# 128 unused bytes ahead of the tiles of h: where the normalised activations begin in SBUF, in a two-layer trunk on one core

## The chip, the cores and the metric

The kernel runs on one core of a Trainium2 chip. The metric is the device time of one execution in microseconds (us), the median over runs.

## What is computed

Two decoder layers over 256 positions of 1024 channels, in float32. Each layer is a half-step SwiGLU FFN, a mixer, and a second half-step FFN; each sublayer has an RMS norm whose output is scaled and shifted by vectors that come from a conditioning row. Layer 0 mixes by causal pooling, layer 1 by attention to K and V that are computed once from the output of layer 0. Since SEQ is 256 and a block has 256 positions, the attention is plain causal attention over one block.

```python
def swiglu(h, w_in, w_out):
    g, u = jnp.split(h @ w_in, 2, axis=-1)          # w_in 1024 x 5632
    return (jax.nn.silu(g) * u) @ w_out             # w_out 2816 x 1024
...
x = x + 0.5 * (1.0 + g)[:, None, :] * swiglu(modulate(rms_norm(x, n), sh, sc), w_in, w_out)   # four times
...
k, v = jnp.split(hn @ w_kv, 2, axis=-1)             # once, after layer 0; hn is "h of shared K/V"
```

## The kernel before, in words

Everything is transposed: channels lie on the 128 partitions, the 256 positions on the free axis, so that h is a tile of 128 x 8 x 256 (`KT` = 8 blocks of channels).

**Three matmuls for one product.** Every operand of a large product is split into a rounded part `hi` and the rest `lo` (ACT casts, L167 and L128; DVE subtracts, L168 and L129), and `mm3` issues three matmuls for each product. The first operand after the output is the stationary one (128 columns, "the weights" of a matmul, loaded anew for every matmul), the second the moving one (256 columns):

```python
    def mm3(o, wh, wl, xh, xl, start, stop):
        i = nc.tensor.matmul(o, wh, xh, ...)             # L255
        nc.tensor.matmul(o[:, 0:T], wh, xl, ...)         # L258
        nc.tensor.matmul(o, wl, xh, ...)                 # L259
```

**The four FFNs.** The weights stream from HBM into raw tiles and are split into tiles of the pool `wp`: stream A (2048 wide: the first product) and stream B (1024 wide: the second). A *gu unit* (`gstep`, L461 ff.) is 48 matmuls: two halves of 8 blocks of channels, three matmuls each; all 24 of a half add into one half of a PSUM tile, and the moving tile (a slice of `hhi` or `hlo`) changes with each block. A *y unit* (`ystep`, L478 ff.) is 24 matmuls: 8 output blocks, three each, with one moving tile pair `acth`, `actl` throughout, and the output changes after every three. `ffn_rest` alternates them: in most of an FFN one gu unit, then one y unit. The first channels of FFNs 2 to 4 are computed ahead from x itself (`gu<-xah`, `gu<-xal`, 258 columns, tiles `kxhi`, `kxlo`), while the norm is being worked out. At the end of an FFN its last y products (96 matmuls) run without gu units between them.

In layer 1, `pj` are the K and Q products (moving tile `hkvh`, `hkvl` or `hhi`, `hlo`; stationary tiles of stream A), `v` the V products (here `hkvh`, `hkvl` are stationary and the tiles of stream A move), `s`, `att` the products of the attention itself, and `y<-hhi` in L1000 the output projection (stationary tiles of stream B, moving `hhi`, `hlo`, which hold the attention's output by head), in the same order of outputs as a y unit.

DVE and ACT do the splits, the norms, the activations and the modulation's dot products (`mod_dot`, L263, from tiles `rawX`, `rawA`, `kxhi`, `kxlo` that are loaded from `in_ada`). SP issues the loads. TensorE's and SP's order is the program's; some stretches of DVE and ACT are ordered by hand, the rest by a scheduler.

**Where tiles lie.** Pools are laid out one after the other in each partition of SBUF, in the order in which they are opened, and tiles in a pool in the order in which their tags are first asked for. Two small tiles that nothing reads stand for room alone:

```python
    ax = ctx.enter_context(tc.tile_pool(name="ax", bufs=8))     # acth, actl
    cp = ctx.enter_context(tc.tile_pool(name="cp", bufs=1))     # constants, x, kxhi, kxlo
    wp = ctx.enter_context(tc.tile_pool(name="wp", bufs=2))     # raw, hi, lo of the two streams
    tp = ctx.enter_context(tc.tile_pool(name="tp", bufs=2))
    hp = ctx.enter_context(tc.tile_pool(name="hp", bufs=1))     # hhi, hlo
    ...
    ax.tile([P, 16], F32, tag="room0", name="room0", bufs=1)
    ...
    cp.tile([P, 16], F32, tag="room1", name="room1")
```

After `hp` come `xp` (`rawX` and the pooling matrix `at`, in layer 0) and in its place later `ap` (`hkvh`, `hkvl`, and the attention's `qh`, `ql`, `ph`, `pl`). In the built program the first bytes of the tiles that TensorE reads are, modulo 256:

| tile | pool | first byte mod 256 | minus the stream's tiles |
|---|---|---|---|
| hi, lo of streams A and B | wp | 160 | 0 |
| acth, actl (all 16 buffers) | ax | 192 | +32 |
| kxhi (xah, kh) / kxlo (xal, kl) | cp | 32 / 96 | +128 / +192 |
| hhi, hlo | hp | 64 | +160 |
| hkvh, hkvl, qh, ql, ph, pl | ap | 64 | +160 |

Every slice that a matmul takes of a stream tile begins a multiple of 512 bytes into it, and every slice of `hhi`, `hlo`, `acth`, `actl`, `hkvh`, `hkvl` a multiple of 512 bytes into that. So the last column holds for each single matmul of its kind, at any block of channels. (Slices of `kxhi` and `kxlo` lie 1032 bytes apart, so theirs grows by 8 with each block.) In a `v` product the roles are changed: what moves lies at 160 and what is stationary at 64, +96.

Of the kernel before, what the change touches and what calls it, by code (L numbers as in the profile page):

```python
# [7 lines left out]
F32 = mybir.dt.float32  # L8
# [5 lines left out]
P = 128  # L14
# [72 lines left out]
def trunk(ctx: ExitStack, tc: tile.TileContext, xin, cin, small, ada, kvada, win0a, win1a, win0b,  # L87
# [7 lines left out]
    hp = ctx.enter_context(tc.tile_pool(name="hp", bufs=1))  # L95
# [2 lines left out]


    ax.tile([P, 16], F32, tag="room0", name="room0", bufs=1)  # L100

    uid = [0]

# [1047 lines left out]
```

## Time and profile before

| | |
|---|---|
| median of 3 runs | 906.83 us (906.48 to 907.52) |
| the profiled execution's own time | 906.3 us |
| its span, first to last instruction | 904.2 us |
| TensorE (PE) busy | 890.9 us, 99% |
| its weight loads (PEld) | 884.3 us, 98% |
| DVE / ACT / POOL busy | 717.4 / 452.5 / 49.2 us |
| HBM read | 238.11 MB, 265 GB/s over the span |

Matmuls are pipelined: a row gives one a duration of 0.28 us, while the next starts about 0.12 us after it. The time that a stretch of matmuls takes is therefore read from starts: the start of the first matmul after it minus the start of its first, divided by their number. This is called the *pitch* below. In the timeline, the columns are the start in us from the span's start, the duration in us, engine, line, operation, output<-inputs, shapes and count.

### The profile page before, as it was taken

The page shows a single profiled execution, that of the slowest core. Times are in us where ns is not written, and L with a number is a line of the kernel's source. Part 1 is how long each engine was busy: PE and PEld are TensorE (multiplying, and loading weights), DVE is VectorE, ACT ScalarE, POOL GpSimd, SP SyncE. Part 2 cuts the span into 40 slices and gives each one's busy share as a digit, 9 for nine tenths or more (in the row PEclk, how much of TensorE's full clock was granted, in tenths as well). Part 3 has the DMA queues.
Part 4 walks back from the last instruction along what each step waited for, and adds up shares of the span by engine and source line. Part 5 has one row for each costly group of instructions (what it writes and reads, how often), then busy time and mean ns, then how long its engine had stood idle before and what let it go on. Part 6 is the DMA issues. An engine that isn't in the chain of part 4 may idle for free.

```text
span 904.2 us, 17826 instructions
## 1 busy us (share of the span) xinstructions
PE 890.9 (99%) x7398; PEld 884.3 (98%) x7398; DVE 717.4 (79%) x1212; ACT 452.5 (50%) x721; POOL 49.2 (5%) x52
## 2 busy tenths in 40 slices
PE   6999999999999999999999999999999999999998
PEld 4999999999999999999999999999999999999998
DVE  5988988878998878869998888789887894665553
ACT  3455344328734444457554443456676674343431
POOL 0000000002000000000000000034431100000000
PEclk9999999999999999999999999999999999999999
DMA  9987998784799998454989899664534376645421
GB/s 354 420 328 288 418 370 345 275 327 147 279 421 400 365 328 323 167 199 165 366 313 391 323 370 358 233 234 184 175 106 132 112 274 253 236 165 205 165 71 47
DMA packets 41699, 240.32 MB, mean 266 GB/s; under 512 B 4625, under 2 KB 5009, under 8 KB 20370
## 3 DMA queue, kind: packets, MB, share of 16 engines
q1 hardware_dynamic: 41618, 239.18, 69.7%
q8 instruction: 58, 0.95, 0.4%
q14 instruction: 23, 0.19, 0.1%
HBM read 238.11 MB, written 1.05 MB: 265 GB/s over the span
## 4 chain that ended last, share of the span: by engine, by line
PE 93%; DVE 4%; DMA 1%; ACT 1%; POOL 1%; issue 0%; DVEq 0%; SPq 0%; POOLq 0%
PE gu L259 18%; PE gu L255 18%; PE gu L258 18%; PE y L258 10%; PE y L255 10%; PE y L259 10%; DVE lo L168 1%; PE gu L720 1%; PE pj L255 1%; PE pj L258 1%; PE pj L259 1%; DMA rawA<-in_ada_dram 1%; PE z L796 1%; DVE rawA L263 1%; POOL r L343 1%
## 5 line engine op out<-in xcount | busy, mean ns | idle before, releaser
L167 ACT CAST hi<-raw 128x1024 fp32r<-128x1024 f32 (+1 forms) x322 | 302.1, 973 | 338.1 <-PE gu L258 224.4
L168 DVE TENSOR_TENSOR lo<-raw,hi 128x1024 fp32r<-128x1024 f32 (+1 forms) x322 | 355.4, 1131 | 135.9 <-ACT hi L167 132.6
L259 PE MATMUL gu<-hhi,lo 128*128 128x256 f32 x1248 | 351.9, 282 | 0.0
L255 PE MATMUL gu<-hhi,hi 128*128 128x256 f32 x1248 | 351.9, 282 | 0.0
L258 PE MATMUL gu<-hlo,hi 128*128 128x256 f32 x1248 | 351.9, 282 | 0.0
L259 PEld LDWEIGHTS gu<-hhi,lo 128*128 128x128 f32 x1248 | 237.5, 190 | 0.2 <-DVE lo L168 0.2
L258 PEld LDWEIGHTS gu<-hlo,hi 128*128 128x128 f32 x1248 | 237.3, 190 | 0.0
L255 PEld LDWEIGHTS gu<-hhi,hi 128*128 128x128 f32 x1248 | 237.2, 190 | 0.0
L255 PE MATMUL y<-acth,hi 128*128 128x256 f32 x704 | 196.4, 279 | 0.0
L259 PE MATMUL y<-acth,lo 128*128 128x256 f32 x704 | 196.3, 279 | 0.0
L258 PE MATMUL y<-actl,hi 128*128 128x256 f32 x704 | 196.3, 279 | 0.0
L255 PEld LDWEIGHTS y<-acth,hi 128*128 128x128 f32 x704 | 132.6, 188 | 0.0
L258 PEld LDWEIGHTS y<-actl,hi 128*128 128x128 f32 x704 | 132.5, 188 | 0.0
L259 PEld LDWEIGHTS y<-acth,lo 128*128 128x128 f32 x704 | 132.3, 188 | 0.0
L263 DVE CUSTOM_DVE_ANT_0 rawX<-rawX,cb 128x1024 f32<-128x1024 f32 x80 | 94.6, 1219 | 0.1
L416 ACT ACTIVATE sl<-gu 128x256 f32<-128x256 f32 x79 | 29.4, 377 | 39.3 <-PE gu L259 37.3
L417 DVE TENSOR_TENSOR sl<-gu,sl 128x256 f32<-128x256 f32 x79 | 32.7, 417 | 14.0 <-ACT sl L416 14.0
L255 PE MATMUL gu<-xah,hi 128*128 128x258 f32 x144 | 41.3, 287 | 0.0
L259 PE MATMUL gu<-xah,lo 128*128 128x258 f32 x144 | 40.7, 282 | 0.0
L258 PE MATMUL gu<-xal,hi 128*128 128x256 f32 x144 | 40.7, 282 | 0.0
L128 ACT CAST acth<-sl 128x256 fp32r<-128x256 f32 x79 | 31.8, 405 | 11.4 <-DVE sl L417 9.9
L129 DVE TENSOR_TENSOR actl<-sl,acth 128x256 fp32r<-128x256 f32 x79 | 32.8, 418 | 1.6 <-ACT acth L128 1.6
(146 smaller groups left out, 1000.0 us busy)
## 6 DMA issues: line engine op xcount, KB each, us to landing
raw<-in_win1b_dram SPq DMA_DIRECT2D x57, 1024.0 KB, 5.3
raw<-in_wout_dram SPq DMA_DIRECT2D x88, 512.0 KB, 5.9
rawX<-in_ada_dram SPq DMA_DIRECT2D x34, 1024.0 KB, 8.6
raw<-in_win1a_dram SPq DMA_DIRECT2D x14, 1024.0 KB, 9.7
rawA<-in_ada_dram SPq DMA_DIRECT2D x12, 1024.0 KB, 6.9
kxhi<-in_ada_dram SPq DMA_DIRECT2D x11, 1024.0 KB, 7.5
kxlo<-in_ada_dram SPq DMA_DIRECT2D x10, 1024.0 KB, 8.7
raw<-in_win0b_dram SPq DMA_DIRECT2D x12, 768.0 KB, 4.2
```

What stands on the lines that cost most here:

```text
L128: i = nc.scalar.copy(hi, src)
L129: nc.vector.tensor_tensor(lo, src, hi.bitcast(F32), op=ALU.subtract)
L167: return [(lambda a=a, b=b: after_anchor(nc.scalar.copy(hi[:, a:b], raw[:, a:b])), lambda a=a, b=b: nc.vector.tensor_tensor(lo[:, a:b], ra ...
L168: lambda a=a, b=b: nc.vector.tensor_tensor(lo[:, a:b], raw[:, a:b], hi[:, a:b].bitcast(F32), op=ALU.subtract)) for a, b in cut]
L255: i = nc.tensor.matmul(o, wh, xh, start=start, stop=False, skip_group_check=True)
L258: nc.tensor.matmul(o[:, 0:T], wh, xl, start=False, stop=False, skip_group_check=True)
L259: nc.tensor.matmul(o, wl, xh, start=False, stop=stop, skip_group_check=True)
L263: i = nc.vector.tensor_tensor_reduce(out=v, in0=v, in1=cb, scale=1.0, scalar=0.0, op0=ALU.mult, op1=ALU.add, accum_out=mb[:, col:col + 1])
L343: nc.gpsimd.tensor_tensor(r, ms, nhalf[:, :n], op=ALU.pow)
L416: nc.scalar.activation(sl, ps[:, 0:T], AF.Silu)
L417: nc.vector.tensor_mul(sl, ps[:, T:2 * T], sl)
L720: nc.tensor.matmul(g0[j][:, half * T:(half + 1) * T], w0[:, (2 * j + half) * P:(2 * j + half + 1) * P], h0, start=(half == 0), stop=False, ...
```

## The change

One unused tile of 32 float32 in each partition (128 bytes) is asked for first in the pool `hp`:

```diff
     ax.tile([P, 16], F32, tag="room0", name="room0", bufs=1)
+    hp.tile([P, 32], F32, tag="room2", name="room2")
 
     uid = [0]
```

`hhi`, `hlo` and everything in `xp` and `ap` begin 128 bytes later: at 192 modulo 256, where they began at 64. Nothing else moves. On every engine the instructions, their order and what they wait for are the same as before; below L99 the line numbers are larger by one.

| tile | minus the stream's tiles, before | after |
|---|---|---|
| hhi, hlo, hkvh, hkvl | +160 | +32 |
| acth, actl | +32 | +32 |
| kxhi / kxlo | +128 / +192 | the same |
| a `v` product (moving minus stationary) | +96 | +224 |

In the attention, `s` (moving kh or kl, stationary qh or ql) and `att` (moving ph or pl, stationary acth or actl) change by 128 as well: 48 matmuls each.

## Rows read from the trace of the kernel before

**Rows 1.** The page: PE's line, and the chain that ended last by engine.
```profile
PE 890.9 (99%) x7398; PEld 884.3 (98%) x7398; DVE 717.4 (79%) x1212; ACT 452.5 (50%) x721; POOL 49.2 (5%) x52
...
PE 93%; DVE 4%; DMA 1%; ACT 1%; POOL 1%; issue 0%; DVEq 0%; SPq 0%; POOLq 0%
```
**Rows 2.** Waits of the weight loads for split weights: us in total, times, longest.
```profile
PEld gu L259 <- DVE lo L168: 0.2, 1, 0.2
```
**Rows 3.** Timeline of PE, FFN 2: a gu unit begins, a y unit, a gu unit.
```profile
299.60 0.28 PE L255 MATMUL gu<-hhi,hi 128*128 128x256 f32 x1
...
305.36 0.28 PE L255 MATMUL y<-acth,hi 128*128 128x256 f32 x1
...
308.16 0.28 PE L255 MATMUL gu<-hhi,hi 128*128 128x256 f32 x1
```
**Rows 4.** Timeline of PE, output projection: two blocks of 24 and what follows each.
```profile
684.48 0.28 PE L255 MATMUL y<-hhi,hi 128*128 128x256 f32 x1
...
687.34 0.27 PE L982 MATMUL pT<-ident,p 128*128 128x128 f32 x1
...
689.08 0.28 PE L255 MATMUL y<-hhi,hi 128*128 128x256 f32 x1
...
691.90 0.28 PE L255 MATMUL att<-ph,acth 128*128 128x256 f32 x1
```
**Rows 5.** Timeline of PE: first y unit and next gu unit, FFNs 2 and 3.
```profile
245.62 0.28 PE L255 MATMUL y<-acth,hi 128*128 128x256 f32 x1
...
248.42 0.28 PE L255 MATMUL gu<-hhi,hi 128*128 128x256 f32 x1
...
254.06 0.28 PE L255 MATMUL y<-acth,hi 128*128 128x256 f32 x1
...
434.34 0.28 PE L255 MATMUL y<-acth,hi 128*128 128x256 f32 x1
...
437.17 0.28 PE L255 MATMUL gu<-hhi,hi 128*128 128x256 f32 x1
...
442.87 0.28 PE L255 MATMUL y<-acth,hi 128*128 128x256 f32 x1
```
**Rows 6.** Timeline of PE: ends of FFN 1's first h block and of the steady stretches.
```profile
24.06 0.28 PE L255 MATMUL gu<-hhi,hi 128*128 128x256 f32 x1
...
74.40 0.28 PE L255 MATMUL y<-acth,hi 128*128 128x256 f32 x1
...
96.94 0.28 PE L255 MATMUL gu<-hhi,hi 128*128 128x256 f32 x1
...
193.74 0.28 PE L255 MATMUL y<-acth,hi 128*128 128x256 f32 x1
...
265.36 0.28 PE L255 MATMUL gu<-hhi,hi 128*128 128x256 f32 x1
...
393.76 0.28 PE L255 MATMUL y<-acth,hi 128*128 128x256 f32 x1
...
445.67 0.28 PE L255 MATMUL gu<-hhi,hi 128*128 128x256 f32 x1
...
582.63 0.28 PE L255 MATMUL y<-acth,hi 128*128 128x256 f32 x1
```
**Rows 7.** Timeline of PE: a block of 48 v products, and the first pj after it.
```profile
593.87 0.28 PE L255 MATMUL v<-hi,hkvh 128*128 128x256 f32 x1
...
599.61 0.28 PE L255 MATMUL pj<-hkvh,hi 128*128 128x256 f32 x1
```
**Rows 8.** Busy time by stretch, FFN 3: us, PE, PEld, DVE, ACT, POOL, PEclk, DMA share, GB/s.
```profile
446.00:582.00 136.00, 136.00 (x1146) 136.00 (x1145) 118.61 (x180) 60.61 (x86) 0.00 (x0) 1.00 0.87 332
```
**Rows 9.** DVE's dot products by tile (L263): duration ns min/median/max.
```profile
L263 DVE CUSTOM_DVE_ANT_0 rawX<-rawX,cb x80: 1207/1219/1226, 9.1 to 366.2; 128x1024 f32<-128x1024 f32 x80
L263 DVE CUSTOM_DVE_ANT_0 kxhi<-kxhi,cb x24: 1212/1218/1221, 268.1 to 807.0; 128x1024 f32<-128x1024 f32 x24
```

## The prediction, made before the run

> **What bounds the kernel.** I read the page first: PE is busy 99% of the span, and the chain that ended last is PE for 93% of it [rows 1]. Next the waits: over the whole run the weight loads wait 0.2 us for split weights [rows 2]. So the time is the number of matmuls times their pitch, and almost nothing else. The windows come third: in the FFN that loads the other engines most, PE is busy 136 of 136 us at the full granted clock (1.00, the 2.4 GHz level), DVE 118.61 of 136 (87%), DMA 0.87 [rows 8]. The change neither adds nor removes an instruction; it can only act through the pitch, so the timeline of PE is what the prediction rests on.
>
> There the reader sees two pitches. The gu unit from 299.60 to 305.36 has 48 matmuls: 5.76 us / 48 = 120.0 ns. The y unit behind it, to 308.16, has 24: 2.80 / 24 = 116.7 ns [rows 3]. Both have 256 moving columns, 128 stationary ones, and no wait. They differ in two ways: gu adds 24 times into one output with a new moving tile for each three, and its moving tile lies 160 bytes beyond the stationary one modulo 256, that of y 32.
>
> **Which of the two it is.** The attention's output projection separates them: it runs in the order of a y unit, but its moving tile is `hhi`, at +160. Its blocks of 24 take 687.34 − 684.48 = 2.86 us (119.2 ns) and 691.90 − 689.08 = 2.82 us (117.5 ns) [rows 4]. The gu units show the same two values where they are not at 120: 254.06 − 248.42 = 5.64 us / 48 = 117.5 ns in FFN 2, and 442.87 − 437.17 = 5.70 / 48 = 118.75 ns in FFN 3 [rows 5]. At +160, then, I see three levels, 117.5, about 119 and 120, for either order of work. At +32 I see two: 116.7 (245.62 to 248.42, 2.80 us / 24) and, in FFN 3's first y unit, 117.9 (434.34 to 437.17, 2.83 / 24) [rows 5]. So the pitch goes with the offset, not with the order of work, and with something that the stretch carries along, a phase between the two reads. FFN 1 and 2 enter in the low level of their offset, FFN 3 in the higher one (and FFN 4 likewise). From the third gu unit of each FFN on, after two changes between +160 and +32, every gu unit stands at 120.0 and every y unit at 116.7.
>
> A rule of the skill speaks against this reading. The Trainium skill, "SBUF — State Buffer", section "Who interferes with whom", says that PE has two independent SBUF read ports, one for the moving operand and one for the weight loads, and that PE never waits on anyone. By it an address could not matter and the time would stay. [Rows 4] disagree in so far as the same order of work runs slower at +160; what it would give here stands among the rivals.
>
> **The change part by part.** The new tile is never written, and costs no instruction. What it does is to put `hhi`, `hlo`, `hkvh`, `hkvl` at +32, where `acth` lies.
>
> (1) *Steady gu units.* The stretches run from 96.94 to 193.74 (10 gu units and 336 y matmuls: 480 × 120.0 + 336 × 116.7 ns = 96.8 us, as measured), 265.36 to 393.76 (15 units, 360 y: 128.4 us), and 445.67 to 582.63 (16 units, 384 y: 137.0 us) [rows 6]; FFN 4 is built as FFN 3. That is 480 + 720 + 768 + 768 = 2736 matmuls at 120.0. At 116.7 each saves 3.3 ns: −9.0 us.
>
> (2) *h blocks near an entry.* FFN 1's first block takes 74.40 − 24.06 = 50.34 us for 429 matmuls, 117.3 ns [rows 6]; at 116.7, −0.28. FFN 1 has 48 more at 117.5 and 48 at about 119 (−0.13), FFN 2 144 at 117.5 and 48 at about 119 (−0.21). FFNs 3 and 4 have 144 each at 118.75, and in the higher level of +32 (117.9) they save 0.12 each. Together −0.86.
>
> (3) *Layer 1's projections.* 384 `pj` and 192 `y<-hhi` matmuls, between 117.5 and 119.2 now [rows 4]: about 1 ns each, −0.6. The start of this stage hangs on DVE, not on PE, so I take half: −0.3.
>
> (4) *FFNs 3 and 4 stay in the level in which they enter.* Before, the shift between +160 and +32 moved them out of it after two units. After the change h and act lie at one offset, and nothing shifts. So I let FFN 3 and 4 run at 117.9 throughout: the 1536 steady gu matmuls save 2.1 ns and not 3.3 (+1.84), and their 960 later y matmuls rise from 116.7 to 117.9 (+1.15). This is my choice; the bounds follow from it.
>
> (5) *Products with an offset that no row shows*: 192 `v` (+96 to +224), 48 `s` and 48 `att`. The nearest row is `v` itself, 599.61 − 593.87 = 5.74 us / 48 = 119.6 ns [rows 7]. All rows of unpaused blocks lie between 116.7 and 120.0, so 288 matmuls may gain 2.9 ns or lose 0.4: −0.8 to +0.1. I take 0, since the nearest row lies at the upper end, and allow ±0.8.
>
> (6) *What else moves.* `rawX` begins 128 bytes later for its loads and for DVE's dot products. These take 1219 ns from `rawX` and 1218 from `kxhi`, which lies elsewhere modulo 256 [rows 9]: nothing. `xah` and `xal` stay.
>
> *Cover.* A steady gu and y pair shrinks from 8.56 to about 8.40 us. DVE's share in FFN 3 rises from 87 to 89%, that of DMA from 0.87 to 0.89 [rows 8], so I let neither take any of it back. Late next would be DVE's split of the weights, whose 0.2 us [rows 2] falls at a transition between stages.
>
> The sum: −9.03 − 0.86 − 0.3 + 1.84 + 1.15 = −7.2 us against the profiled execution's own 906.3 (span 904.2): 899.1. The median of the runs is 0.5 above that execution, so I give **899.6**.
>
> **The rivals.**
> - *All four FFNs in the low level.* Then (4) falls away and the entries of 3 and 4 save 0.35 more: −10.5, 896.3. For it: from the third unit on all y units stand at 116.7. Against: two of four enter at the higher level.
> - *All four in the higher level.* FFN 1 and 2 lose 1.2 ns on 1200 gu matmuls (1.4), on 2 × 528 y matmuls (1.3) and on their entries (0.9): −3.6, 903.2.
> - *No effect of the address.* If the 120 belongs to the work of a gu unit (24 adds into one output) and not to the offset, nothing moves: 906.8. [Rows 4] speak against it. It is also the result of the skill's rule on the two ports.
> - *Slower: y loses its level and gu gains nothing.* The place is the steady alternation. If y reaches 116.7 only because a gu unit at another offset hands over its phase, and h locks at 120 whatever its offset, then with one offset for both all 2112 y matmuls run at 117.9, 2.5 us more: 909.3. It decides if the steady gu pitch stays above 119.1 ns (2.5 us over 2736 matmuls is 0.9 ns). For it: FFN 3's first y unit at 117.9 [rows 5] before any such exchange. Against: FFN 2's first at 116.7.
> - *The feeds take it back.* If FFN 3, with DVE at 87%, kept its 137 us, its part of the sum (768 × 2.1 − 480 × 1.2 ns = 1.0 us) would be lost: 900.6, in the range.
> - *The tile doesn't move h.* The built program has h 128 bytes later, so I give this nothing.
>
> **How the numbers follow.** Forecast (some FFNs low, some high) 0.46; all low 0.25; all high 0.08; fed too slowly 0.04; no effect 0.10; slower 0.07. The range reaches from all low with the gain of (5), 896.3 − 0.8 = 895.5, to all high with its loss, 903.2 + 0.8 = 904.0; what is left out is no effect, slower, and a little beside them. A measurement of this kernel tells 0.2% (1.8 us) from no change. Faster by more: 0.46 + 0.25 + 0.08 + 0.04 = 0.83; same 0.10; slower 0.07.
>
> **What would show it.** In the timeline, a gu unit of FFN 2 should take 5.60 us (116.7 ns) or 5.66 (117.9) in place of 5.76, and the y unit beside it should be at the same pitch. FFN 3's steady 137.0 us should be about 135.8 if it is in the higher level, 134.4 if low; FFN 1's 96.8 should be 95.2. The count of matmuls, DVE's 1219 ns and the granted clock should not change. It is wrong if gu units stay at 120.0, if they take another pitch than 116.7 or 117.9, or if they reach it and PE then waits for DVE or DMA in steady stretches.

## The result, and the profile after

The changed kernel takes 896.96 us (median of 4 runs, 894.96 to 899.96) against 906.79 before (906.48 to 907.52): a ratio of 0.9893, 95% interval 0.9864 to 0.9922. Timed once more (v_after, below) it took 895.98 us (894.64 to 897.02), ratio 0.9883 (0.9866 to 0.9900). The forecast was 899.6 us in a range of 895.5 to 904.0, and faster with 0.83.

The profiled execution of the changed kernel took 894.96 us, the quickest of the first four; its span is 892.8 us where that of before was 904.2. First the page after: PE's line, and the chain by engine. They answer to [rows 1].

```profile
PE 879.4 (99%) x7398; PEld 873.0 (98%) x7398; DVE 717.1 (80%) x1212; ACT 453.0 (51%) x721; POOL 49.4 (6%) x52
...
PE 93%; DVE 4%; DMA 1%; ACT 1%; POOL 1%; issue 0%; DVEq 0%; SPq 0%; POOLq 0%
```

The same 7398 matmuls and 1212 DVE instructions, the same shares of the chain, 11.5 us less of PE. DVE's and ACT's busy time is unchanged within 0.5 us: nothing but the matmuls became cheaper.

The timeline of PE after, FFNs 1 to 4. The rows answer to [rows 3, 6]: FFN 1's first h block (first two rows), ends of the steady stretches, and in FFN 2 a gu unit, a y unit, a gu unit.

```profile
23.64 0.28 PE L256 MATMUL gu<-hhi,hi 128*128 128x256 f32 x1
...
73.69 0.28 PE L256 MATMUL y<-acth,hi 128*128 128x256 f32 x1
...
96.09 0.28 PE L256 MATMUL gu<-hhi,hi 128*128 128x256 f32 x1
...
191.29 0.28 PE L256 MATMUL y<-acth,hi 128*128 128x256 f32 x1
...
262.72 0.28 PE L256 MATMUL gu<-hhi,hi 128*128 128x256 f32 x1
...
287.92 0.28 PE L256 MATMUL gu<-hhi,hi 128*128 128x256 f32 x1
...
293.52 0.28 PE L256 MATMUL y<-acth,hi 128*128 128x256 f32 x1
...
296.32 0.28 PE L256 MATMUL gu<-hhi,hi 128*128 128x256 f32 x1
...
388.72 0.28 PE L256 MATMUL y<-acth,hi 128*128 128x256 f32 x1
...
440.30 0.28 PE L256 MATMUL gu<-hhi,hi 128*128 128x256 f32 x1
...
574.70 0.28 PE L256 MATMUL y<-acth,hi 128*128 128x256 f32 x1
...
743.00 0.28 PE L256 MATMUL gu<-hhi,hi 128*128 128x256 f32 x1
...
877.40 0.28 PE L256 MATMUL y<-acth,hi 128*128 128x256 f32 x1
```

FFN 4's steady stretch before, for which [rows 6] have no row:

```profile
751.86 0.28 PE L255 MATMUL gu<-hhi,hi 128*128 128x256 f32 x1
...
888.81 0.28 PE L255 MATMUL y<-acth,hi 128*128 128x256 f32 x1
```

The gu unit takes 293.52 − 287.92 = 5.60 us for 48 matmuls, 116.7 ns where it was 120.0; the y unit 2.80 us for 24, 116.7 ns as before. The steady stretches take 95.20, 126.00, 134.40 and 134.40 us. Against 96.80, 128.40 and 136.96 of before [rows 6], with FFN 4 before at 136.95, that is 9.1 us less. The span fell by 11.4. Of the other 2.3 us, 0.42 lie ahead of FFN 1's first h block (it begins at 23.64 and began at 24.06), where the moved tiles play no part; in v_after, the same kernel once more, the block began at 24.09, so these 0.42 us are no gain of the change. 0.43 lie between that and FFN 1's steady stretch, and 0.2, 0.3 and 0.9 in the three stretches between the steady ones.

Busy time in FFN 3's stretch after (us, PE, PEld, DVE, ACT, POOL, granted clock, DMA share, GB/s); it answers to [rows 8].

```profile
441.00:574.00 133.00, 133.00 (x1142) 133.00 (x1141) 118.08 (x179) 60.50 (x86) 0.00 (x0) 1.00 0.89 339
```

PE is still busy all of it, at the same granted clock (1.00), with DVE now at 118.08 of 133 (89%) and DMA at 0.89. The feeds took nothing back.

### The profile page after: what moved, and what is told of

Read it like the earlier page. It is cut to its first block, busy times and chain, and to the rows that moved or that the text cites. A ratio compares the mean times of both kernels' runs of the same rounds, so it can differ in the third digit from the quotient of the medians.

```text
span 892.8 us, 17826 instructions
## 1 busy us (share of the span) xinstructions
PE 879.4 (99%) x7398; PEld 873.0 (98%) x7398; DVE 717.1 (80%) x1212; ACT 453.0 (51%) x721; POOL 49.4 (6%) x52
## 4 chain that ended last, share of the span: by engine, by line
PE 93%; DVE 4%; DMA 1%; ACT 1%; POOL 1%; issue 0%; DVEq 0%; SPq 0%; POOLq 0%
PE gu L256 18%; PE gu L260 18%; PE gu L259 18%; PE y L259 10%; PE y L256 10%; PE y L260 10%; DVE lo L169 1%; PE gu L721 1%; PE pj L256 1%; PE pj L259 1%; PE pj L260 1%; DMA rawA<-in_ada_dram 1%; PE z L797 1%; DVE rawA L264 1%; POOL r L344 1%
## 5 line engine op out<-in xcount | busy, mean ns | idle before, releaser
L256 PE MATMUL gu<-hhi,hi 128*128 128x256 f32 x1248 | 348.4, 279 | 0.0
L260 PE MATMUL gu<-hhi,lo 128*128 128x256 f32 x1248 | 348.3, 279 | 0.0
L259 PE MATMUL gu<-hlo,hi 128*128 128x256 f32 x1248 | 348.2, 279 | 0.0
L260 PEld LDWEIGHTS gu<-hhi,lo 128*128 128x128 f32 x1248 | 234.6, 188 | 0.1
L256 PEld LDWEIGHTS gu<-hhi,hi 128*128 128x128 f32 x1248 | 234.6, 188 | 0.0
L259 PEld LDWEIGHTS gu<-hlo,hi 128*128 128x128 f32 x1248 | 234.6, 188 | 0.0
L264 DVE CUSTOM_DVE_ANT_0 rawX<-rawX,cb 128x1024 f32<-128x1024 f32 x80 | 94.6, 1219 | 0.4 <-DMA rawX<-in_ada_dram 0.4
L129 ACT CAST acth<-sl 128x256 fp32r<-128x256 f32 x79 | 31.9, 406 | 13.1 <-DVE sl L418 11.4
```

What stands on the lines that cost most here:

```text
L129: i = nc.scalar.copy(hi, src)
L256: i = nc.tensor.matmul(o, wh, xh, start=start, stop=False, skip_group_check=True)
L259: nc.tensor.matmul(o[:, 0:T], wh, xl, start=False, stop=False, skip_group_check=True)
L260: nc.tensor.matmul(o, wl, xh, start=False, stop=stop, skip_group_check=True)
L264: i = nc.vector.tensor_tensor_reduce(out=v, in0=v, in1=cb, scale=1.0, scalar=0.0, op0=ALU.mult, op1=ALU.add, accum_out=mb[:, col:col + 1])
```

## The experiments

Theory A: a matmul's pitch goes with the distance modulo 256 between the first bytes of its moving and its stationary tile, and at each distance has a few levels. Theory B: the gain comes from what lies behind h. Theory C: it comes from the address of h itself. The kernel before ran again beside each group of runs; a ratio compares the runs with those beside them, and is not the quotient of two medians of the table. Times from one run carry no interval. The offsets in the table are those from the tiles of the two weight streams, modulo 256; gu and y are the pitches in steady units of the four FFNs in the profiled execution.

| run | h | act | us (runs) | ratio to before | gu, ns | y, ns |
|---|---|---|---|---|---|---|
| before | 160 | 32 | 906.79 (4) | | 120.0 | 116.7 |
| the change | 32 | 32 | 896.96 (4) | 0.9893 (0.9864 to 0.9922) | 116.7 | 116.7 |
| v_after, the change again | 32 | 32 | 895.98 (4) | 0.9883 (0.9866 to 0.9900) | 116.7; FFN 2 117.8 | 116.7; FFN 2 117.8 |
| e1_h_only | 32 | 32 | 895.30 (4) | 0.9877 (0.9861 to 0.9894) | 116.7 | 116.7 |
| e2_kv_only | 160 | 32 | 906.88 (10) | 1.0003 (0.9993 to 1.0012) | 120.0; FFN 2 118.7 | 116.7 |
| e3_plus384 | 32 | 32 | 897.10 (1) | | 116.7 | 116.7 |
| e4_both160 | 160 | 160 | 905.69 (10) | 1.0004 (0.9987 to 1.0021) | FFN 1 120.0, others 118.7 | the same as gu |
| s_h0 | 0 | 32 | 911.94 (1) | | 119.9 | 118.0 |
| s_h64 | 64 | 32 | 893.80 (1) | | FFNs 1, 2 113.4; 3, 4 117.8 | 116.9, 117.1; 116.6 |
| s_h96 | 96 | 32 | 908.85 (1) | | 119.8 to 119.9 | 118.1 in FFN 1, 116.6 |
| s_h224 | 224 | 32 | 903.35 (1) | | 118.3 | 116.9 |
| b_64_64 | 64 | 64 | 896.68 (5) | 0.9914 (0.9879 to 0.9948) | 117.8 | 117.8 |
| b_64_192 | 64 | 192 | 897.57 (5) | 0.9912 (0.9884 to 0.9939) | 117.8 | FFN 1 113.5, others 117.6 to 117.7 |
| v_h64, s_h64 again | 64 | 32 | 894.63 (4) | 0.9864 (0.9847 to 0.9880) | FFNs 1, 2 113.4; 3, 4 117.8 | 116.9, 117.1; 116.6 |

**e1_h_only: h alone is moved.** From the changed kernel, a second unused tile behind h puts all that follows back to where it was modulo 256.

```diff
     hp.tile([P, 32], F32, tag="room2", name="room2")
...
             h = new_h("h")
+            hp.tile([P, 32], F32, tag="room3", name="room3")
```

> Only hhi and hlo lie at +32; a second unused tile behind them leaves hkvh, hkvl, rawX and the tiles of the attention where before had them modulo 256 (+160). Theory A (the offset between the moving and the stationary tile of a matmul sets its pitch): gu units of the four FFNs at 116.7 ns, or 117.9 in an FFN that falls into the higher level; the 192 pj matmuls on hkvh, hkvl stay at 117.4 to 118.8 and the v blocks near 119.8, as before; the time 0.5 to 1 us above the change, 896 to 900 us. Theory B (the gain comes from what lies behind h: the loads' tiles or the shared K/V): gu units stay at 120.0 and the time near 906.8.

895.30 us (894.49 to 895.79). The timeline of PE, FFN 2, and below it a block of 48 v products with the first pj behind it:

```profile
288.47 0.28 PE L256 MATMUL gu<-hhi,hi 128*128 128x256 f32 x1
...
294.07 0.28 PE L256 MATMUL y<-acth,hi 128*128 128x256 f32 x1
...
586.46 0.28 PE L256 MATMUL v<-hi,hkvh 128*128 128x256 f32 x1
...
592.21 0.28 PE L256 MATMUL pj<-hkvh,hi 128*128 128x256 f32 x1
```

gu units 5.60 us, 116.7 ns; v stays at 5.75 us / 48 = 119.8 ns, where the change has 118.3. The whole gain is there without shared K/V; the 0.5 to 1 us that I had put on shared K/V are not, and the time lies below the 896 to 900 that I expected. Theory B falls.

**e2_kv_only: the complement.** The unused tile behind h alone, from the kernel before.

```diff
             h = new_h("h")
+            hp.tile([P, 32], F32, tag="room3", name="room3")
```

> The complement: hhi and hlo stay at +160, everything behind them moves by 128 bytes as in the change. Theory A: gu units at 120.0 from the third of each FFN on, pj on hkvh, hkvl at 116.7 to 117.9 and v blocks near 118.3; the time 0 to 1 us under before, 905.8 to 906.8. Theory B: the time near 897.

906.88 us, ratio 1.0003 (0.9993 to 1.0012). The timeline of PE: a gu unit of FFN 2, one of FFN 3, and a block of v:

```profile
275.23 0.28 PE L255 MATMUL gu<-hhi,hi 128*128 128x256 f32 x1
...
280.93 0.28 PE L255 MATMUL y<-acth,hi 128*128 128x256 f32 x1
...
471.81 0.28 PE L255 MATMUL gu<-hhi,hi 128*128 128x256 f32 x1
...
477.57 0.28 PE L255 MATMUL y<-acth,hi 128*128 128x256 f32 x1
...
594.30 0.28 PE L255 MATMUL v<-hi,hkvh 128*128 128x256 f32 x1
...
599.98 0.28 PE L255 MATMUL pj<-hkvh,hi 128*128 128x256 f32 x1
```

In FFNs 1, 3 and 4 gu is at 5.76 us, 120.0 ns, as before. The v blocks did become shorter (5.68 us / 48 = 118.3 ns against 119.6 before [rows 7]), and three of the four pj blocks on hkvh fell to 116.6 to 116.8 (without the one gap of some 0.2 us that three of the blocks hold), yet the time did not move. The trace shows one reason: behind these products PE waits for POOL, before and after the change alike. The rows are those of the kernel before and of the change, with the wait in brackets:

```profile
634.25 0.65 PE L349 MATMUL rbk<-ident,r 128*128 128x128 f32 x4 [1.84 <-POOL r L343]
...
626.21 0.65 PE L350 MATMUL rbk<-ident,r 128*128 128x128 f32 x4 [2.09 <-POOL r L344]
```

From the start of FFN 3's last y products (582.63 and 574.70) to these rows it is 51.62 and 51.51 us: with the change the wait grew by 0.25 us and the stretch shrank by 0.11, so the wait takes most of what these products save.

One thing was not as expected: in FFN 2 gu stayed at 118.7 in every unit of this execution (5.70 us above), and never reached 120, although its units alternated between +160 and +32.

**e3_plus384: is the period 256?** 384 bytes in place of 128, so that h is 32 beyond the weights modulo 256 but 288 modulo 512.

```diff
-    hp.tile([P, 32], F32, tag="room2", name="room2")
+    hp.tile([P, 96], F32, tag="room2", name="room2")
```

> The unused tile has 384 bytes in place of 128: h is again 32 beyond the weights modulo 256, but 288 modulo 512 (the change has 32, the activations 288). Theory A with a period of 256 bytes: gu units at 116.7 (or 117.9 in an FFN), 895 to 900 us. Rival (period of 512 or more): gu units at another pitch than 116.7 or 117.9.

897.10 us in one run. The timeline of PE, a gu unit of FFN 2, and the window from 626 to 630 us (us, PE, PEld, DVE, ACT, POOL, granted clock, DMA share, GB/s):

```profile
288.48 0.28 PE L256 MATMUL gu<-hhi,hi 128*128 128x256 f32 x1
...
294.08 0.28 PE L256 MATMUL y<-acth,hi 128*128 128x256 f32 x1
...
626.00:630.00 4.00, 3.33 (x16) 3.33 (x17) 3.65 (x7) 3.11 (x5) 2.02 (x2) 0.58 0.74 262
```

5.60 us, 116.7 ns; gu and y are at 116.7 in all four FFNs. For this distance it makes no difference whether h lies 32 or 288 beyond. All FFNs are in the low level as in the first execution of the change, and yet the time is 2.1 us longer. 0.5 us lie ahead of FFN 1's first h block, and 1.6 in layer 1: there PE, after a wait of 2.0 us for POOL, runs at a mean granted clock of 0.58, for the most part at the lower of its two levels (1.2 GHz), and its matmuls start 0.21 us apart in place of 0.12. In the first execution of the change the same place, after a wait of 2.1 us, shows 1.00. So a time alone does not tell how many FFNs are in the high level.

**e4_both160: the distance or the address?** 128 more bytes behind the activations, from the kernel before. The weights and h move up by them: h comes to lie at 192 modulo 256, as in the change, but still 160 from the weights, and the activations now lie 160 from the weights too.

```diff
-    cp.tile([P, 16], F32, tag="room1", name="room1")
+    cp.tile([P, 48], F32, tag="room1", name="room1")
```

> From the kernel before, 128 more unused bytes behind the activations' tiles: acth, actl now lie at +160 from the weights, as h does; h itself, the weights and all else behind lie 128 bytes further up, with the same offsets among themselves. Theory A1 (the offset sets the levels, and only the alternation between two offsets drives the phase up to 120): gu and y units all stay at the level in which an FFN enters, 117.4 or 118.7; 901 to 907.5 us. Theory A2 (at +160 a stretch settles at 120 by itself): gu and y both at 120.0, 913 to 914 us. Theory C (it is the address of h itself, 192 modulo 256, not its distance from the weights): gu units at 116.7, 896 to 900 us.

905.69 us (903.83 to 910.42). The timeline of PE, FFN 1 (first two rows) and FFN 2:

```profile
119.21 0.28 PE L255 MATMUL gu<-hhi,hi 128*128 128x256 f32 x1
...
124.97 0.28 PE L255 MATMUL y<-acth,hi 128*128 128x256 f32 x1
...
294.86 0.28 PE L255 MATMUL gu<-hhi,hi 128*128 128x256 f32 x1
...
300.56 0.28 PE L255 MATMUL y<-acth,hi 128*128 128x256 f32 x1
...
303.40 0.28 PE L255 MATMUL gu<-hhi,hi 128*128 128x256 f32 x1
```

FFN 1: 5.76 us / 48 = 120.0 ns. FFN 2: gu 5.70 / 48 = 118.75, y 2.84 / 24 = 118.3 (118.7 over all its units). The address of h is the same as in the change and the pitch is not: theory C falls. The y units, at 116.7 for as long as their tile lay at +32, now run at the pitch of the gu units. That is the other half of the case for theory A: the order of work of a y unit does not make it quick. The median agrees with A1 (901 to 907.5) and not with A2 (913 to 914); three of the ten runs lie above A1's range, this execution (910.27) among them. In its detail A1 was wrong: FFN 1 sat at 120.0 without any alternation of offsets.

**s_h0, s_h64, s_h96, s_h224: other distances.** The unused tile has 96, 160, 192 and 64 bytes.

```diff
-    hp.tile([P, 32], F32, tag="room2", name="room2")
+    hp.tile([P, 24], F32, tag="room2", name="room2")
```

The others have 40, 48 and 16 in place of 24.

> The unused tile has 96 bytes: h and shared K/V begin exactly at the weights modulo 256 (offset 0), the activations stay at +32. What each offset gives was not known for this one. Theory A (each offset has its own few levels of pitch, +32 those at 116.7 and 117.9): gu units at some other level, between 116 and 126 ns, y units at 116.7 to 117.9; 895 to 925 us. Rival A' (only +160, half a period from +32, is slow): gu at 116.7, about 897 us.

> The unused tile has 160 bytes: h and shared K/V at +64, the activations at +32. Theory A: gu units at a level of their own between 116 and 122 ns; y units at 116.7 to 117.9; 895 to 912 us. Rival A': gu at 116.7, about 897 us.

> The unused tile has 192 bytes: h and shared K/V at +96. Before had the v products at this offset, in another role, at 119.8 ns. Theory A: gu units at 118 to 121 ns, 900 to 910 us. Rival A': gu at 116.7, about 897 us.

> The unused tile has 64 bytes: h and shared K/V at +224 (32 short of the weights). After the change the v products have this offset, in another role, at 118.3 ns. Theory A: gu units at 117 to 121 ns, 898 to 910 us. Rival A': gu at 116.7, about 897 us.

911.94, 893.80, 908.85 and 903.35 us; the one run of the kernel before beside them took 904.65. The timeline of PE with h at 0, FFN 2:

```profile
294.30 0.28 PE L256 MATMUL gu<-hhi,hi 128*128 128x256 f32 x1
...
300.05 0.28 PE L256 MATMUL y<-acth,hi 128*128 128x256 f32 x1
...
302.88 0.28 PE L256 MATMUL gu<-hhi,hi 128*128 128x256 f32 x1
```

gu is 5.75 us / 48 = 119.8 ns, and y rises to 2.83 / 24 = 117.9 (118.0 over all its units), near the higher level of its own +32, although nothing about its tiles changed: its level depends on the units between which it runs. The timeline with h at +64, FFN 2 and FFN 3:

```profile
293.34 0.28 PE L256 MATMUL gu<-hhi,hi 128*128 128x256 f32 x1
...
298.79 0.28 PE L256 MATMUL y<-acth,hi 128*128 128x256 f32 x1
...
469.67 0.28 PE L256 MATMUL gu<-hhi,hi 128*128 128x256 f32 x1
...
475.32 0.28 PE L256 MATMUL y<-acth,hi 128*128 128x256 f32 x1
```

5.45 us / 48 = 113.5 ns in FFN 2, and 5.65 / 48 = 117.7 ns in FFN 3, in one execution, with the same code and the same offsets. So a distance does not give one pitch, it gives a set of levels, and +64 has one well below all that was known, below the 116 to 122 ns and the 895 to 912 us that I expected of theory A. At the other three the pitches lie in theory A's ranges, which were wide. Rival A' falls at 0, 96 and 224, and at 64 too.

**b_64_64 and b_64_192: does that level hold?** h at +64, the activations at +64 or at +192.

```diff
-    hp.tile([P, 32], F32, tag="room2", name="room2")
+    hp.tile([P, 40], F32, tag="room2", name="room2")
...
-    cp.tile([P, 16], F32, tag="room1", name="room1")
+    cp.tile([P, 8], F32, tag="room1", name="room1")
```

This is b_64_64 against the changed kernel; b_64_192 has 40 in place of the 8.

> h, shared K/V and the activations all at +64, the offset at which gu units stood at 113.4 ns in FFNs 1 and 2 and at 117.8 in FFNs 3 and 4 of the look at h alone. Theory A1 (offset sets the levels, and with one offset an FFN keeps the level in which it enters): gu and y units of an FFN at the same pitch, 113.4 or 117.8; all low 877 us, two of four low 890, none low 903, and the runs some 6 us apart from one another. Rival (113.4 came of the alternation between +64 and +32): gu and y units all at 117.8, 903 us in every run.

> h and shared K/V at +64, the activations at +192, half a period further, so that the two alternate as +160 and +32 did in the kernel before. At +192 two of four v blocks stood at 113.6 ns in the look with h at +64. Theory A1 with the alternation as it was before (the shift by half a period drives every FFN into one level by its third gu unit): all four FFNs alike; if into the low level 877 us, if into the high one 903 us. Rival (the alternation fixes nothing): FFNs differ among themselves as they did with the activations at +32, about 890 us.

896.68 us (896.06 to 903.74) and 897.57 (895.15 to 901.73). The timeline of b_64_64, FFN 2, and a block of v with the first pj after it:

```profile
299.71 0.28 PE L256 MATMUL gu<-hhi,hi 128*128 128x256 f32 x1
...
305.36 0.28 PE L256 MATMUL y<-acth,hi 128*128 128x256 f32 x1
...
308.19 0.28 PE L256 MATMUL gu<-hhi,hi 128*128 128x256 f32 x1
...
591.84 0.28 PE L256 MATMUL v<-hi,hkvh 128*128 128x256 f32 x1
...
597.29 0.28 PE L256 MATMUL pj<-hkvh,hi 128*128 128x256 f32 x1
```

gu 117.7 ns and y 2.83 / 24 = 117.9, in all four FFNs of this execution, which took 903.74 us, close to what was expected of "none low" (903); in the same execution a v block, whose distance is here +192, takes 5.45 / 48 = 113.5. The other four runs took 896.06, 896.23, 896.68 and 902.43, steps that fit one FFN in the low level or none; none of those was profiled, so this is argued and not shown. b_64_192 refutes the expectation that a shift by half a period drives all FFNs into one level: in FFN 1 its y units stand at 113.5 beside gu at 117.8, in the others at 117.6 to 117.7. Its time met neither the 877 or 903 of theory A1 nor the 890 of the rival. Neither kernel is shown to be quicker than the change.

**v_h64 and v_after: the best two, side by side.** The kernels of s_h64 and of the change, timed together.

> The kernel of the look at h +64 and activations +32 again, now timed against the kernel before. Theory A1 (an FFN keeps the level in which it enters, and the entry differs from run to run): gu at 113.4 with y at 117.2, or gu at 117.8 with y at 116.6; all four FFNs low 886 us, none low 900 us, the runs scattered between, the median about 895. Rival (FFNs 1 and 2 always enter low, 3 and 4 never): 893 to 895 us in every run.

> The changed kernel again, on the same chip as the run beside it. Theory A1: between about 895 us (all four FFNs at 116.7) and 902 us (all at 117.9), some 1.7 us for each FFN that enters the higher level, median 895 to 898. Rival (the scatter of the first four runs was the chip's): all runs within 0.3% of each other as the kernel before has them, near 896.

894.63 us (893.30 to 895.29) and 895.98 (894.64 to 897.02). The intervals overlap, so +64 is not shown to beat +32. v_h64 repeats the pattern of s_h64 in the steady stretches: FFNs 1 and 2 low, 3 and 4 high; the four runs lie within the 893 to 895 us (to the rounding) that the rival named, so here, unlike b_64_64, the steady levels seem to be the same in every run. The entry is not: FFN 1's first h block (429 matmuls, as in [rows 6]) ran at 113.3 ns in s_h64 and at 117.8 in v_h64, and both stood at 113.4 from the third gu unit on. The timeline of v_after, FFN 2 with the ends of its steady stretch, and FFN 3:

```profile
263.49 0.28 PE L256 MATMUL gu<-hhi,hi 128*128 128x256 f32 x1
...
288.93 0.28 PE L256 MATMUL gu<-hhi,hi 128*128 128x256 f32 x1
...
294.59 0.28 PE L256 MATMUL y<-acth,hi 128*128 128x256 f32 x1
...
297.41 0.28 PE L256 MATMUL gu<-hhi,hi 128*128 128x256 f32 x1
...
390.69 0.28 PE L256 MATMUL y<-acth,hi 128*128 128x256 f32 x1
...
467.56 0.28 PE L256 MATMUL gu<-hhi,hi 128*128 128x256 f32 x1
...
473.16 0.28 PE L256 MATMUL y<-acth,hi 128*128 128x256 f32 x1
```

FFN 2 is at 5.66 us / 48 = 117.9 and 2.82 / 24 = 117.5 ns (117.8 over its steady stretch), the higher level of +32; FFN 3 at 116.7. In the first execution FFN 2 was at 116.7. So with one program an FFN can fall into either level, and stays in it to its end: FFN 2's steady stretch took 127.20 us here and 126.00 there. This execution took 897.02 us against 894.96: with FFN 2's entry and end the level makes 1.6 of the 2.1 us, and 0.45 lie ahead of FFN 1's first h block. The times of the four runs do not decide between theory A1 and its rival: they lie within 0.27% of each other near 896, as the rival said, and also between the 895 and 902 of theory A1. The trace of FFN 2 decides that the level can differ.

## Why the prediction was right, point by point

- *What bounds the kernel.* Right. PE's share and the chain are the same after, and all but 0.4 of the 11.4 us lie where the pitch fell.
- *Offset and not order of work.* Right, and now shown from three sides: h alone moved (e1), everything else moved (e2), and y slowed by its own offset (e4). The "phase between the two reads" that the prediction names is a picture for the levels; no run shows what it is.
- *The rule on two independent read ports.* The Trainium skill, "SBUF — State Buffer", section "Who interferes with whom", says that PE's two read ports are independent and that PE never waits on anyone; the prediction concluded from this that an address could not matter. Here the gu pitch went from 120.0 to 116.7 ns, and with other distances to 113.4 or 119.9, with the same instructions and no wait. The measurement decides: for this stream of weight loads and matmuls the distance of the two operands does matter. Which part of the chip makes it so was not tested.
- *(1) Steady gu units, −9.0.* The four stretches fell by 9.1 us in the profiled execution. Right to 0.1. (Before, in FFNs 1 and 2, the third gu unit still stood at 118.7 and the fourth was the first at 120.0; the text of the prediction says the third, its sum has it right.)
- *(2) Entries, −0.86.* FFN 1 fell by 0.43 between its first h block and its steady stretch, where 0.41 was forecast; the first block alone by 0.29 (50.34 to 50.05), where 0.28 was. FFN 2's entry fell by 0.19 (0.21). FFNs 3 and 4 entered low and not high, and fell by 0.33 and 0.34, where 0.12 each was forecast and 0.3 each for the low level. Right, but for the level that (4) chose.
- *(3) Layer 1's projections, −0.3.* The layer fell by 0.6: 0.1 ahead of the end of PE's wait for POOL, and 0.5 behind it. By their pitches the pj and y products on `hhi` make some 0.4 of that 0.5, and two blocks of v, which (5) put at nothing, some 0.1. Leaving out the products on shared K/V was right, for the wait takes their gain (e2); the term was too small by some 0.1 for the rest.
- *(4) FFNs 3 and 4 stay in the level in which they enter, +3.0.* This is the step that failed. Half of it holds: with one offset an FFN does keep its level. But which level it enters was read off one execution of the kernel before and carried over, and the entry into +32 is not that into +160. In the profiled execution all four were low, in v_after only FFN 2 was high. Nor is the shift between +160 and +32 needed to bring an FFN to 120, or enough: FFN 1 of e4 stood there with one offset, and FFN 2 of e2 never came there in spite of the shift. Without this term the sum is −10.2 against 906.3, and the execution fell by 11.3. The rival "all four in the low level", 896.3, came nearer to the two medians than the forecast did. The levels of the other three of the first four runs are not known, since none of them was profiled. Two of them (896.62 and 897.30) need no high FFN: their mean granted clock was 0.997, as in e3, which took 897.10 with all four low. The third (899.96, clock 0.998) is 2.9 us above e3, more than one high FFN makes in v_after. The result lies in the range all the same, because the range also held "all four low", not because of this step.
- *(5) Unknown offsets, 0 ± 0.8.* v moved from 119.6 to 118.3 ns at +224; in e2, where it did the same, no gain in time was seen. Well within the ±0.8.
- *(6) What else moves.* The dot products from `rawX` take 1219 ns at both places, as [rows 9]: for these reads of DVE the place made no difference. The row after is this, with duration in ns, min/median/max:

```profile
L264 DVE CUSTOM_DVE_ANT_0 rawX<-rawX,cb x80: 1212/1219/1227, 8.9 to 361.8; 128x1024 f32<-128x1024 f32 x80
```

- *The slower rival* said that h might lock at 120 wherever it lay. It did not at +32. But what it feared for y does happen elsewhere: with h at 0, the y units lost their level (118.0 in place of 116.7) and the time rose to 911.94.

What stays open: what it is that a stretch carries, what decides the level at an entry, and whether the 113.4 ns of +64 can be held through a whole execution. No run tried to steer it.

## What to carry to other kernels

Where TensorE is the bound and every matmul loads its weights anew, read the pitch from the starts of neighbouring matmuls by kind of operand: if two kinds with the same shapes and no waits differ by a few per cent, compare where their moving and stationary tiles begin modulo 256. All this was seen with one shape, 128 stationary and 256 moving columns. Some unused bytes ahead of a pool test it without one instruction more, but the best distance has to be measured, and over several executions, since one distance can have two or three levels. A difference of 0.2% between two runs of such a kernel may be the level of one FFN (1.6 us in v_after), or a few us at the lower clock (1.6 us in e3): only the trace tells which.

## What had not been expected of the hardware

- At one distance a stretch of matmuls keeps one of several steady pitches, in one execution of one program: 113.4 and 117.8 ns at +64, 116.7 and 117.8 at +32, 118.7 and 120.0 at +160.
- The level can differ from run to run of one program: FFN 2's steady stretch took 126.00 us in one execution of the changed kernel and 127.20 in another. Whether this widened the scatter of the runs is not shown: the first four runs of the changed kernel lie 5.0 us apart and the four of the kernel before beside them 1.0, but four more of the changed kernel lie 2.4 apart (894.64 to 897.02), and the seven of the kernel before beside those 3.7 (904.26 to 907.95).
- After a wait of PE of some 2 us in layer 1 the granted clock fell in some executions and not in others: to 0.58 from 626 to 630 us in e3, while the same place of the changed kernel, after a wait as long, shows 1.00.
- 113.4 ns is 5.5% below the 120.0 of the kernel before at the same granted clock (1.00 in both stretches), so the 116.7 that both products now have is not a floor of this sequence.
